# Bias transposes spread over four steps, and the retention's transposes and halves set one step later

## The chip, the cores and the metric

The kernel runs on one core of one Trainium2 chip. The metric is the device time of one execution in microseconds, from a profile-free timing; three runs of the kernel before are given. The profile is one further execution, recorded by the hardware profiler.

## The reference, cut to what matters

One layer of a streaming encoder: x (256 frames of 2048 channels) passes a SwiGLU feed-forward block, then a mixing stage, then a second feed-forward block and a last norm. All of it is float32. Only the mixing stage matters here:

```
proj = rmsnorm(x) @ w_in                       # q_a k_a v_a q_r k_r v_r g_r gate_a gate_r
scores = q_a k_a^T * hd**-0.5 + bias           # 8 heads of 128; bias = rel_bias[clip(q - k)]
att = softmax(masked scores) v_a               # chunks of 64 frames see earlier chunks only
q_r, k_r = rotary(q_r), rotary(k_r)
ret = (q_r k_r^T * decay) v_r                  # 8 heads, no softmax
ret = silu(g_r) * ret / rms(ret)               # rms over one head's 128 channels
merged = sigmoid(gate_a) * (att @ w_out_att) + sigmoid(gate_r) * (ret @ w_out_ret)
x = x + merged @ w_out
```

## The kernel before, in words

**Products in three parts.** Every large product splits both operands into a high and a low float32r part and multiplies three times (`three`, lines 130 to 132: high by high, low weight by high, high weight by low). Weights come in blocks of 256 rows by 512 columns on SyncE's queue (`fetch`, L116), ScalarE rounds a block to its high part (L122), and VectorE subtracts it to get the low part (L123).

**Steps.** A step is one such weight block. An ordinary step (`standard`) multiplies it with both frame tiles t = 0 and 1, first all six matmuls of t = 0 into one accumulator bank, then six of t = 1 into another. Before the matmuls of step c, `run` first issues the split of the weight block of step c + 3 (four split buffers, so this split waits for the end of step c - 1 on TensorE), and then the functions that are due in step c. `later(n, fn)` puts a function into the list of the step that is n steps after the current one; a list is worked off in the order in which its entries were made. All engines take their instructions in this order, so the order of the work is written out by these calls and nothing reorders it. When the last step of a job is issued, its `done` function is called, which evicts the accumulators.

**Banks.** TensorE writes to eight PSUM banks in three groups: three with the tag acc, three with the tag z (`acc_tile`), and two side banks (`side_tile`). A new tile gets a bank of its tag when one of those before it has been read for the last time; its first matmul waits for that on TensorE, in front of all later matmuls.

**The stretch in question.** The mixing stage's projection to the second half of v_r begins at the step called `mixed` in the code; here the steps are counted from it, so that `mixed` is step 0. The order of jobs is: v_r second half, steps 0 to 7; q_r heads 0 to 3, 8 to 15; k_r heads 0 to 3, 16 to 23; q_r heads 4 to 7, 24 to 31; k_r heads 4 to 7, 32 to 39; then att @ w_out_att, four jobs of four steps (blocks 0 to 3 of the result's columns), 40 to 55; ret @ w_out_ret, four jobs of four steps, 56 to 71; and merged @ w_out from 72. Each job of steps 40 to 71 takes one bank acc for t = 0 and one bank z for t = 1; attention's are evicted by VectorE (`branch_a_done`, L1027, into siga).

Small work is hung into these steps:

- The bias. Its transposed table is read from DRAM in two tiles (biasT, four heads each). `bias_natural` runs in step 0: for each pair of heads four transposes on TensorE into a side bank (psb, L326) and a copy by ScalarE (L331); at the end VectorE fills the corner that is masked (L333).
- Attention, head h of 8: the scores in step 4 + 4h (L854, L855 into the side bank as; VectorE's scaling plus bias at L862 reads it), exponentials in step 5 + 4h, the division in 6 + 4h, the transposes of the weights in step 8 + 4h (L890 into the side bank apt, copied by ScalarE at L892), the values in step 10 + 4h (L898, L899 into the side bank av, split by L343 and L344).
- The retention's queries and keys. `ret_qk_done` runs at the end of step 15 (q_r, heads 0 to 3: qr0), 23 (kr0), 31 (qr1) and 39 (kr1). ScalarE scales the two accumulators, VectorE turns them (rotary, L815 to L818) one and two steps later, and `to_transposed` transposes them four steps later (19, 27, 35, 43): four transposes per frame tile into a side bank (qr0p and so on, L349), copied by ScalarE for t = 0 (L784) and by VectorE for t = 1 (L786).
- The retention itself, `retention(b)`, for heads 4b to 4b + 3, is put into the lists at the end of kr0 (step 23) and kr1 (step 39). RET_WAIT is (14, 5). Scores of head i: L923, L924 into the side bank rs, multiplied with the decay by VectorE (L926, L927 into rp), in steps 37, 39, 41, 43 for b = 0 and 44, 46, 48, 50 for b = 1. Values three steps later (L936 to L938), all four heads into one pair of accumulators (ro, one bank acc and one bank z), which are taken with the first head's values, in step 40 and step 47. `finish` runs in step 46 and step 53: ScalarE squares the accumulators, VectorE sums the squares (L948), GpSimd takes the power (L340), and VectorE scales the accumulators by it and by the gate (rg, L954), first for t = 0, then for t = 1. Three steps later, in step 49 and step 56, `ret.put` transposes the result (retp, L349), ScalarE rounds it to the high part (reth, L343) and VectorE subtracts (retl, L344).
- The result of heads 0 to 3 is block 0 of the operand ret and is used from step 56 on; that of heads 4 to 7 is block 1 and is first used in step 58.

The lines that set these distances:

```
HALF_K = D // P // 2
RET_WAIT = (14, 5)
...
            to_transposed(key, b, srcs, 4)
...
            later(3, lambda: [ret.put(b, t, srcs[t]) for t in range(NT)])

        for i in range(4):
            for s, stage in enumerate(head(i)):
                later(wait + 2 * i + 3 * s, stage)
        later(wait + 2 * 4 + 1, finish)
```

Of the kernel before, what the change touches and what calls it, by code (L numbers as in the profile page):

```python
# [15 lines left out]
P = 128  # L16
SEQ = 256
NT = SEQ // P
D = 2048
DFF = 5632  # L20
CHUNK = 64
HEADS = 8
# [7 lines left out]
MASKED = -1e30  # L30
# [7 lines left out]
HALF_K = D // P // 2  # L38
LEAD = 12
MIX_LEAD = 8  # L40
RET_WAIT = (14, 5)
HELD = 6

SHARE = (0.85,) * 4 + (1.0,) * 4 + (0.8,) + (0.4,) * 3 + (0.15,) * 4
# [27 lines left out]
def block_kernel(ctx: ExitStack, tc: tile.TileContext, x, g1, w1g, w1u, w1d, gm, w_in, rel, woa, wor, wo,  # L72
                 g2, w2g, w2u, w2d, gf, cos, sin, decay, ident, out):
    nc = tc.nc
# [10 lines left out]
    def act_tile(dt, name):  # L85
        return apool.tile([P, 4, SEQ], dt, tag="act", name=name)

    def acc_tile(name, tag="acc"):
        return psum.tile([P, NB], F32, tag=tag, name=name, bufs=3)

    def side_tile(name):
        return psum.tile([P, NB], F32, tag="side", name=name, bufs=2)

    def tmp_tile(name, tag="t", bufs=None):
        return tmp.tile([P, NB], F32, tag=tag, name=name, bufs=bufs)
# [9 lines left out]
    def later(n, fn):  # L105
        due.setdefault(state["step"] + n, []).append(fn)
# [151 lines left out]
    def load_gain(g, i, queue=nc.gpsimd):  # L258
        rows = small.tile([D // P, P], F32, tag="rows", name=f"grows{i}", bufs=1)
        queue.dma_start(rows, g[0].rearrange("(k p) -> k p", p=P))  # L260

        def turn():
            ps = side_tile(f"gps{i}")
            nc.tensor.transpose(ps[:, : D // P], rows, id_sb[: D // P, : D // P])
            nc.vector.tensor_copy(gains[:, i, :], ps[:, : D // P])

        return turn
# [8 lines left out]
    table = {}  # L276
# [42 lines left out]
    def bias_natural(bt):  # L319
        for b in range(HEADS // 4):  # L320
            table["bias", b] = act_tile(F32, f"bias{b}")
        for h in range(0, HEADS, 2):
            ps = side_tile(f"psb{h}")
            for i in range(2):
                for j in range(2):
                    nc.tensor.transpose(  # L326
                        ps[:, (2 * i + j) * P : (2 * i + j + 1) * P],
                        bt[(h + i) // 4][:, (h + i) % 4, j * P : (j + 1) * P],
                        id_sb,
                    )  # L330
            nc.scalar.copy(table["bias", h // 4][:, h % 4 : h % 4 + 2, :].rearrange("p h k -> p (h k)"), ps)  # L331
        for b in range(HEADS // 4):
            nc.vector.memset(table["bias", b][0:CHUNK, :, CHUNK:P], MASKED)  # L333


    def rsqrt(dst, ssum, n, width):

        v = small.tile([P, width], F32, tag="v", name="v")
        nc.vector.tensor_scalar(v, ssum, 1.0 / n, EPS, op0=ALU.mult, op1=ALU.add)
        nc.gpsimd.tensor_tensor(dst, v, mhalf[:, :width], op=ALU.pow)  # L340
# [5 lines left out]
    def transpose4(src, name):  # L346
        ps = side_tile(name)
        for i in range(4):
            nc.tensor.transpose(ps[:, i * P : (i + 1) * P], src[:, i * P : (i + 1) * P], id_sb)  # L349
        return ps  # L350
# [421 lines left out]
    def heads_t(ts):  # L772
        return slice(ts * P, (ts + 1) * P)

    def to_transposed(key, b, srcs, steps):

        dst = act_tile(F32, f"{key}{b}T")
        tposed[key, b] = dst

        def go():  # L780
            for t in range(NT):
                ps = transpose4(srcs[t], f"{key}{b}p{t}").rearrange("p (i q) -> p i q", i=4)
                if t == 0:
                    nc.scalar.copy(dst[:, :, heads_t(t)], ps)  # L784
                else:
                    nc.vector.tensor_copy(dst[:, :, heads_t(t)], ps)  # L786

        later(steps, go)
# [12 lines left out]
    def ret_qk_done(key, b, after=None):  # L801
        def done(acc):
            srcs = []
            half = HD // 2

            def turn(t, s):
                r = tmp_tile(f"{key}{b}{t}r", "qk", 4)
                u = tmp_tile(f"{key}{b}{t}u", "scaled", 1)
                s4 = s.rearrange("p (h j d) -> p h j d", h=4, j=2)
                r4 = r.rearrange("p (h j d) -> p h j d", h=4, j=2)  # L810
                u4 = u.rearrange("p (h j d) -> p h j d", h=4, j=2)
                c = cos_sb[:, t, :].unsqueeze(1).to_broadcast([P, 4, half])
                n = sin_sb[:, t, :].unsqueeze(1).to_broadcast([P, 4, half])
                for j in range(2):
                    nc.vector.tensor_mul(r4[:, :, j, :], s4[:, :, j, :], c)  # L815
                    nc.vector.tensor_mul(u4[:, :, j, :], s4[:, :, 1 - j, :], n)
                nc.vector.tensor_sub(r4[:, :, 0, :], r4[:, :, 0, :], u4[:, :, 0, :])
                nc.vector.tensor_add(r4[:, :, 1, :], r4[:, :, 1, :], u4[:, :, 1, :])  # L818
                srcs.append(r)


            for t in range(NT):
                s = tmp_tile(f"{key}{b}{t}", "gate", 2)
                nc.scalar.activation(s, acc[t], AF.Copy, scale=nm.scale(t))
                later(1 + t, lambda t=t, s=s: turn(t, s))
            to_transposed(key, b, srcs, 4)
            if after is not None:
                after()

        return done  # L830
# [13 lines left out]
    ret = Operand("ret", HEADS // 4)  # L844
# [65 lines left out]
    def retention(b):  # L910

        wait = RET_WAIT[b]
        outs = {}

        def head(i):
            h = 4 * b + i
            hs = slice(i * HD, (i + 1) * HD)
            sm = {}

            def scores():  # L920
                q, k = tposed["qr", b], tposed["kr", b]
                ps = side_tile(f"rs{h}")
                nc.tensor.matmul(ps[:, 0:SEQ], k[:, i, 0:P], q[:, i, :], start=True, stop=True)  # L923
                nc.tensor.matmul(ps[:, SEQ : SEQ + P], k[:, i, P:SEQ], q[:, i, P:SEQ], start=True, stop=True)  # L924
                s = act_tile(F32, f"rp{h}").rearrange("p a q -> p (a q)")[:, : 3 * P]
                nc.vector.tensor_mul(s[:, :SEQ], ps[:, :SEQ], table["decay", b][:, i, :])  # L926
                nc.vector.tensor_mul(s[:, SEQ:], ps[:, SEQ : SEQ + P], table["decay", b][:, i, 0:P])  # L927
                sm["s"] = s

            def values():  # L930
                if i == 0:
                    for t in range(NT):
                        outs[t] = acc_tile(f"ro{b}{t}", ("acc", "z")[t])
                v = nat["vr", b]
                s = sm["s"]
                nc.tensor.matmul(outs[0][:, hs], s[:, 0:P], v[:, 0, hs], start=True, stop=True)  # L936
                nc.tensor.matmul(outs[1][:, hs], s[:, P:SEQ], v[:, 0, hs], start=True, stop=False)
                nc.tensor.matmul(outs[1][:, hs], s[:, SEQ:], v[:, 1, hs], start=False, stop=True)  # L938

            return scores, values  # L940

        def finish():
            srcs = []
            for t in range(NT):
                sq = tmp_tile(f"rsq{b}{t}", "gate", 2)
                nc.scalar.activation(sq, outs[t], AF.Square)
                ms = small.tile([P, 4], F32, tag="ms", name="ms")
                nc.vector.reduce_sum(ms, sq.rearrange("p (h d) -> p h d", h=4), axis=AX.X)  # L948
                rs = small.tile([P, 4], F32, tag="rs", name="rs")
                rsqrt(rs, ms, HD, 4)  # L950
                o = tmp_tile(f"rg{b}{t}", "qk", 4)
                for i in range(4):
                    hs = slice(i * HD, (i + 1) * HD)
                    nc.vector.scalar_tensor_tensor(  # L954
                        o[:, hs], outs[t][:, hs], rs[:, i : i + 1], nat["gr", b][:, t, hs], op0=ALU.mult, op1=ALU.mult
                    )
                srcs.append(o)
            later(3, lambda: [ret.put(b, t, srcs[t]) for t in range(NT)])

        for i in range(4):  # L960
            for s, stage in enumerate(head(i)):
                later(wait + 2 * i + 3 * s, stage)
        later(wait + 2 * 4 + 1, finish)

    w_in0 = w_in[0]
# [129 lines left out]
    turn = load_gain(g1, 0, nc.scalar)  # L1095
# [41 lines left out]
    def set_bias():  # L1137
        bt = bias_transposed()
        later(4, lambda: bias_natural(bt))
# [75 lines left out]
```

## Time and profile before

| what | value |
|---|---|
| median of three runs | 2105.22 us (2102.99 to 2106.69) |
| the profiled execution's own time | 2105.12 us |
| its span, first to last instruction | 2103.4 us |
| mean granted clock of TensorE | 0.998 of full speed |
| TensorE busy (matmuls) | 2065.5 us, 98% |
| VectorE, ScalarE, GpSimd busy | 1761.1, 1408.4, 273.8 us (84%, 67%, 13%) |
| HBM traffic | 224 GB/s over the span |
| chain of work that ended last | TensorE 77%, VectorE 11%, issue 4%, ScalarE 4%, DMA 3% |

The stretch that the change touches lies between about 1070 and 1270 us of the span. In the rows, a line of the timeline gives the start of an instruction (or of several merged ones) in us from the span's start, its duration in us, engine, line of the kernel, operation, what it writes and reads, and how many were merged; in brackets stands the idle time ahead of it and what ended that. Matmuls are pipelined, so durations of neighbours overlap, and the distance between starts is the rate. PEclk is the granted clock of TensorE as a share of full speed.

### The profile page before, as it was taken

The page shows a single profiled execution, that of the slowest core. Times are in us where ns is not written, and L with a number is a line of the kernel's source. Part 1 is how long each engine was busy: PE and PEld are TensorE (multiplying, and loading weights), DVE is VectorE, ACT ScalarE, POOL GpSimd, SP SyncE. Part 2 cuts the span into 40 slices and gives each one's busy share as a digit, 9 for nine tenths or more (in the row PEclk, how much of TensorE's full clock was granted, in tenths as well). Part 3 has the DMA queues.
Part 4 walks back from the last instruction along what each step waited for, and adds up shares of the span by engine and source line. Part 5 has one row for each costly group of instructions (what it writes and reads, how often), then busy time and mean ns, then how long its engine had stood idle before and what let it go on. Part 6 is the DMA issues. An engine that isn't in the chain of part 4 may idle for free.

```text
span 2103.4 us, 25824 instructions
## 1 busy us (share of the span) xinstructions
PE 2065.5 (98%) x9256; PEld 1688.7 (80%) x9256; DVE 1761.1 (84%) x1825; ACT 1408.4 (67%) x1734; POOL 273.8 (13%) x322
## 2 busy tenths in 40 slices
PE   9999999999999999999999999999999999999998
PEld 7788878888888888878778888887888778888886
DVE  6998899888988799889966667568888988898986
ACT  7677667777777766766664434556776677677785
POOL 1111211122111110121100000010122012110200
PEclk9999999999999999999999999999999999999999
DMA  8667876788678777798776645575787668766873
GB/s 300 192 215 231 276 208 209 229 265 239 197 234 236 244 210 238 255 289 247 220 253 180 214 137 184 187 241 172 229 277 231 192 223 268 236 199 228 279 210 130
DMA packets 219313, 473.27 MB, mean 225 GB/s; under 512 B 14816, under 2 KB 15568, under 8 KB 219184
## 3 DMA queue, kind: packets, MB, share of 16 engines
q1 hardware_dynamic: 161376, 310.42, 44.0%
q0 software_dynamic: 54752, 155.88, 27.4%
q10 hardware_dynamic: 3056, 5.32, 0.7%
q8 instruction: 72, 1.18, 0.2%
q14 instruction: 57, 0.47, 0.1%
HBM read 462.65 MB, written 8.91 MB: 224 GB/s over the span
## 4 chain that ended last, share of the span: by engine, by line
PE 77%; DVE 11%; issue 4%; ACT 4%; DMA 3%; ACTq 0%; POOL 0%; POOLq 0%; DVEq 0%
PE acc L131 15%; PE acc L132 14%; PE acc L130 14%; DVE lo L123 2%; DMA raw<-in_ffn_w_down_dram 2%; ACT hi L122 1%; DMA z992x<-in_ffn_w_gate_dram 1%; DMA rawz24323r<-in_ffn_w_up_dram 1%; ACT xall L733 0%; PE z128a L131 0%; PE z800a L131 0%; PE z205a L130 0%; PE z380a L130 0%; PE z128a L130 0%; PE z800a L130 0%
## 5 line engine op out<-in xcount | busy, mean ns | idle before, releaser
L123 DVE TENSOR_TENSOR lo<-raw,hi 128x1024 fp32r<-128x1024 f32 (+1 forms) x401 | 487.2, 1217 | 176.5 <-ACT hi L122 174.7
L122 ACT CAST hi<-raw 128x1024 fp32r<-128x1024 f32 (+1 forms) x401 | 418.9, 1048 | 230.0 <-PE acc L132 143.7
L730 ACT ACTIVATE acc<-xall 128x512 f32<-128x512 f32 x96 | 57.5, 599 | 8.4 <-DVE f1g L697 3.5
L733 ACT ACTIVATE xall<-acc 128x512 f32<-128x512 f32 x96 | 56.4, 588 | 4.5 <-PE acc L132 3.8
L130 PE MATMUL acc<-hi,mgh 128*128 128x512 f32 x128 | 50.1, 392 | 0.0
L132 PE MATMUL acc<-hi,mgl 128*128 128x512 f32 x128 | 49.8, 389 | 0.0
L131 PE MATMUL acc<-lo,mgh 128*128 128x512 f32 x128 | 49.8, 389 | 0.0
L131 PE MATMUL acc<-lo,nma01h 128*128 128x512 f32 x96 | 38.0, 396 | 1.6 <-DVE lo L123 1.6
L130 PE MATMUL acc<-hi,nma00h 128*128 128x512 f32 x96 | 38.9, 405 | 0.0
L131 PE MATMUL acc<-lo,nma00h 128*128 128x512 f32 x96 | 38.4, 400 | 0.3 <-DVE lo L123 0.3
L130 PE MATMUL acc<-hi,nma01h 128*128 128x512 f32 x96 | 38.5, 401 | 0.0
L132 PE MATMUL acc<-hi,nma00l 128*128 128x512 f32 x96 | 38.0, 396 | 0.0
L130 PE MATMUL acc<-hi,nma10h 128*128 128x512 f32 x96 | 37.7, 393 | 0.0
L131 PE MATMUL acc<-lo,nma10h 128*128 128x512 f32 x96 | 37.6, 392 | 0.0
L132 PE MATMUL acc<-hi,nma01l 128*128 128x512 f32 x96 | 37.6, 391 | 0.0
L132 PE MATMUL acc<-hi,nma10l 128*128 128x512 f32 x96 | 37.5, 390 | 0.0
L132 PE MATMUL acc<-hi,nma11l 128*128 128x512 f32 x96 | 37.4, 390 | 0.0
L130 PE MATMUL acc<-hi,nma11h 128*128 128x512 f32 x96 | 37.4, 390 | 0.0
L131 PE MATMUL acc<-lo,nma11h 128*128 128x512 f32 x96 | 37.4, 389 | 0.0
L132 PEld LDWEIGHTS acc<-hi,mgl 128*128 128x128 f32 x128 | 24.0, 188 | 4.9
L130 PEld LDWEIGHTS acc<-hi,mgh 128*128 128x128 f32 x128 | 24.0, 188 | 4.9
L131 PEld LDWEIGHTS acc<-lo,mgh 128*128 128x128 f32 x128 | 24.0, 188 | 4.9
(6130 smaller groups left out, 7143.9 us busy)
## 6 DMA issues: line engine op xcount, KB each, us to landing
raw<-in_ffn_w_down_dram SPq DMA_DIRECT2D x176, 512.0 KB, 6.2
raw<-in_w_in_dram SPq DMA_DIRECT2D x96, 512.0 KB, 4.4
raw<-in_ffn_w_up_dram SPq DMA_DIRECT2D x32, 512.0 KB, 8.6
raw<-in_w_out_dram SPq DMA_DIRECT2D x32, 512.0 KB, 3.7
raw<-in_ffn_w_gate_dram SPq DMA_DIRECT2D x31, 512.0 KB, 5.7
raw<-in_w_out_att_dram SPq DMA_DIRECT2D x16, 512.0 KB, 3.9
raw<-in_w_out_ret_dram SPq DMA_DIRECT2D x16, 512.0 KB, 3.9
z380x<-in_w_in_dram POOLq DMA_DIRECT2D x8, 512.0 KB, 7.8
```

The costliest lines, as they stand in the source:

```text
L122: nc.scalar.copy(hi[:, p, :], raw[:, p, :])
L123: nc.vector.tensor_sub(lo[:, p, :], raw[:, p, :], hi[:, p, :].bitcast(F32))
L130: nc.tensor.matmul(acc, ahi, whi, start=first, stop=False, **more)
L131: nc.tensor.matmul(acc, ahi, wlo, start=False, stop=False, **more)
L132: nc.tensor.matmul(acc, alo, whi, start=False, stop=last, **more)
L730: nc.scalar.activation(acc, xs[t][:, cols], AF.Copy, scale=2.0)
L733: nc.scalar.activation(xs[t][:, cols], acc, AF.Copy, scale=0.5)
```

## The change

The turn of the bias is split: the pair of heads 0 and 1 is transposed in step 0, pairs 2, 4 and 6 in steps 1, 2 and 3, each with its own masked fill. RET_WAIT becomes (15, 6), so that both halves of the retention (scores, values, finish) start a step later: b = 0 has scores in 38, 40, 42, 44, values in 41, 43, 45, 47 and its finish in 47; b = 1 has scores in 45, 47, 49, 51, values in 48, 50, 52, 54 and its finish in 54. `to_transposed` of the retention's queries and keys runs five steps after the projection's end: 20, 28, 36, 44. `ret.put` runs four steps after its finish, so in 51 and 58. No transfer is added or moved, and the amount of computation is the same.

```diff
--- before.py
+++ after.py
@@ -38,7 +38,7 @@
 HALF_K = D // P // 2
 LEAD = 12
 MIX_LEAD = 8
-RET_WAIT = (14, 5)
+RET_WAIT = (15, 6)
 HELD = 6
 
 SHARE = (0.85,) * 4 + (1.0,) * 4 + (0.8,) + (0.4,) * 3 + (0.15,) * 4
@@ -319,7 +319,8 @@
     def bias_natural(bt):
         for b in range(HEADS // 4):
             table["bias", b] = act_tile(F32, f"bias{b}")
-        for h in range(0, HEADS, 2):
+
+        def turn(h):
             ps = side_tile(f"psb{h}")
             for i in range(2):
                 for j in range(2):
@@ -328,9 +329,13 @@
                         bt[(h + i) // 4][:, (h + i) % 4, j * P : (j + 1) * P],
                         id_sb,
                     )
-            nc.scalar.copy(table["bias", h // 4][:, h % 4 : h % 4 + 2, :].rearrange("p h k -> p (h k)"), ps)
-        for b in range(HEADS // 4):
-            nc.vector.memset(table["bias", b][0:CHUNK, :, CHUNK:P], MASKED)
+            dst = table["bias", h // 4][:, h % 4 : h % 4 + 2, :]
+            nc.scalar.copy(dst.rearrange("p h k -> p (h k)"), ps)
+            nc.vector.memset(dst[0:CHUNK, :, CHUNK:P], MASKED)
+
+        turn(0)
+        for h in range(2, HEADS, 2):
+            later(h // 2, lambda h=h: turn(h))
 
 
     def rsqrt(dst, ssum, n, width):
@@ -823,7 +828,7 @@
                 s = tmp_tile(f"{key}{b}{t}", "gate", 2)
                 nc.scalar.activation(s, acc[t], AF.Copy, scale=nm.scale(t))
                 later(1 + t, lambda t=t, s=s: turn(t, s))
-            to_transposed(key, b, srcs, 4)
+            to_transposed(key, b, srcs, 5)
             if after is not None:
                 after()
 
@@ -955,7 +960,7 @@
                         o[:, hs], outs[t][:, hs], rs[:, i : i + 1], nat["gr", b][:, t, hs], op0=ALU.mult, op1=ALU.mult
                     )
                 srcs.append(o)
-            later(3, lambda: [ret.put(b, t, srcs[t]) for t in range(NT)])
+            later(4, lambda: [ret.put(b, t, srcs[t]) for t in range(NT)])
 
         for i in range(4):
             for s, stage in enumerate(head(i)):
```

## Rows read from the trace of the kernel before

**Rows 1.** The page's busy table: engine, busy us, share, instructions.

```profile
PE 2065.5 (98%) x9256; PEld 1688.7 (80%) x9256; DVE 1761.1 (84%) x1825; ACT 1408.4 (67%) x1734; POOL 273.8 (13%) x322
```

**Rows 2.** Waits of TensorE, 1069 to 1265 us: total, times, longest.

```profile
PE psb L326 <- ACT bias L331: 1.9, 1, 1.9
PE retp L349 <- DVE rp L927: 1.0, 1, 1.0
PE kr1p L349 <- ACT kr1T L784: 0.7, 1, 0.7
...
```

**Rows 3.** Timeline of TensorE, steps 0 and 1.

```profile
1069.95 1.04 PE L326 MATMUL psb<-id_sb,biasT 128*128 128x128 f32 x8
1072.84 1.15 PE L326 MATMUL psb<-id_sb,biasT 128*128 128x128 f32 x8 [1.85 <-ACT bias L331]
1073.74 0.63 PE L130 MATMUL acc<-hi,nma00h 128*128 128x512 f32 x1
...
1078.16 0.39 PE L130 MATMUL acc<-hi,nma00h 128*128 128x512 f32 x1
...
1080.88 0.39 PE L130 MATMUL acc<-hi,nma01h 128*128 128x512 f32 x1
```

**Rows 4.** Windows of TensorE: busy us, PEclk, DMA share, GB/s.

```profile
1238.00:1244.00 6.00, 4.97 (x30) 1.00 0.72 212
1073.74:1077.20 3.46, 3.46 (x12) 0.52 0.97 335
```

**Rows 5.** Timeline of TensorE, step 19.

```profile
1132.91 0.60 PE L349 MATMUL qr0p<-id_sb,qr00r 128*128 128x128 f32 x4
1134.11 0.66 PE L349 MATMUL qr0p<-id_sb,qr01r 128*128 128x128 f32 x4 [0.60 <-DVE attl L344]
1134.52 0.48 PE L130 MATMUL acc<-hi,nma01h 128*128 128x512 f32 x1
```

**Rows 6.** Timeline of TensorE, ScalarE and VectorE, step 28.

```profile
1164.23 0.49 PE L890 MATMUL apt<-id_sb,p 128*128 128x128 f32 x3
...
1165.13 0.47 PE L130 MATMUL acc<-hi,nma00h 128*128 128x512 f32 x1
...
1165.43 0.47 ACT L892 COPY p<-apt 128x384 f32<-128x384 f32 x1
...
1166.70 0.68 DVE L862 SCALAR_TENSOR_TENSOR p<-as,bias 128x128 f32<-128x128 f32 x3
```

**Rows 7.** Timeline of TensorE and VectorE, steps 46 and 47.

```profile
1226.71 0.38 PE L936 MATMUL ro<-vr,rp 128*128 128x128 f32 x2
...
1231.37 0.48 PE L130 MATMUL acc<-hi,atth 128*128 128x512 f32 x1
...
1231.16 1.12 DVE L954 SCALAR_TENSOR_TENSOR rg<-ro,rs,gr 128x128 f32<-128x128 f32 x4 [1.15 <-POOL rs L340]
...
1234.21 1.13 DVE L954 SCALAR_TENSOR_TENSOR rg<-ro,rs,gr 128x128 f32<-128x128 f32 x4 [1.12 <-POOL rs L340]
```

**Rows 8.** Timeline of TensorE and VectorE, step 50.

```profile
1243.15 0.59 PE L923 MATMUL rs<-qr1T,kr1T 128*128 128x256 f32 x2
...
1245.91 0.28 DVE L927 TENSOR_TENSOR rp<-rs,decay 128x128 f32<-128x128 f32 x1
```

**Rows 9.** Timeline of TensorE, VectorE and ScalarE, steps 53 to 56.

```profile
1253.14 0.38 PE L936 MATMUL ro<-vr,rp 128*128 128x128 f32 x2
...
1262.02 1.03 PE L349 MATMUL retp<-id_sb,rg 128*128 128x128 f32 x8
...
1260.61 1.13 DVE L954 SCALAR_TENSOR_TENSOR rg<-ro,rs,gr 128x128 f32<-128x128 f32 x4 [1.12 <-POOL rs L340]
1261.65 2.35 DVE L123 TENSOR_TENSOR lo<-raw,hi 128x1024 fp32r<-128x1024 f32 x2
1263.92 1.28 DVE L1027 TENSOR_TENSOR siga<-acc,siga 128x512 f32<-128x512 f32 x2
...
1263.18 1.07 ACT L343 CAST reth<-retp 128x512 fp32r<-128x512 f32 x2
```

## The prediction

> **What bounds the kernel now.** I read four views. The page's busy table comes first: TensorE is busy for 98% of the span [rows 1], so a change pays only where TensorE stands still or runs slowly. The list of TensorE's waits in the stretch that the change touches comes next [rows 2]: six waits, and each is for a PSUM side bank that a slower engine still has to empty. They are 1.9 us at the bias, 1.0 at the retention's first result (retp), 0.7 at kr1p, and 0.60 three times (qr0p, whose wait stands in [rows 5], kr0p and qr1p): 5.4 us in all. The change moves exactly these six places. Third, TensorE in order of time around the bias shows a second loss [rows 3]: sixteen transposes and a wait fill 1069.95 to 1073.74, and the first eight products that follow are 0.43 us apart where ordinary ones are 0.23 apart. The windows view names it: the granted clock is 0.52 there, the 1.2 GHz level [rows 4]. Last I followed, step by step, who empties the banks that the moved work will ask for.
>
> A step of twelve products takes 2.72 us (1078.16 to 1080.88) [rows 3]; a group of four transposes takes 0.41 (1134.11 to 1134.52) [rows 5]. Steps are numbered as in the description above.
>
> **The bias.** Now step 0 lasts from 1069.95 to 1078.16, 8.21 us [rows 3]; 2.72 are products, 5.49 are the price of the turn. Afterwards one group of four stands in each of steps 0 to 3, 0.41 each plus about 0.08 for the slower first product behind it, 2.0 in all. Each step then needs one side bank, and the copy that frees it has a step's time. Gain **3.5 us**; at the least 1.85, the wait alone. Head 0's scores come at step 4, heads 4 to 7 from step 20, so no score waits for a bias. ScalarE has the same four copies; four smaller fills replace two on VectorE, which waits for ScalarE in these steps anyway; without that cover they cost what the two cost now, about half a microsecond in all.
>
> **Queries and keys, steps 19, 27, 35, 43 to 20, 28, 36, 44.** Steps 20 and 28 already hold an attention head's transposes and the next head's scores, so four side tiles now share two banks. Take step 28 as it is: transposes at 1164.23, products at 1165.13, that is 0.90 in; ScalarE's copy frees the first bank at 1165.90 (1.67 in), VectorE's scaling frees the second at 1167.38 (3.15 in) [rows 6]. The first group can start at 1.7 and end at 2.1; the second needs either the second bank or the first again. A copy behind a first group let the next group start after about 1.3 (0.41 for its transposes, some 0.2 until their end is told, 0.7 the wait at kr1p [rows 2]; the 0.2 is what 1.20 from group to group leaves beside 0.41 and a wait of 0.60 [rows 5]), so 3.0; products follow at 3.4 in place of 0.90, 2.5 more. Taken away is 1.61 (1132.91 to 1134.52) [rows 5] and a little for one break fewer: **+0.8 each, +1.6**. If the banks are handed out the other way round, both groups wait for 3.15 and it is +1.3 each. At step 36 only the head's transposes are in the way: the second group waits to 1.7, products at 2.1 where now three transposes (0.3, three quarters of a group) and 1.61 are paid apart, **+0.2**. Step 44 repeats step 43 (scores, then keys): 0. So these four waits are not lost: VectorE's late release is replaced by a fuller step.
>
> **The retention's first half, steps 37 to 46 become 38 to 47.** No transfer moves with it; GpSimd's power, in the finish, stands behind loads issued long before; the weights' queue is not passed. What moves is the release of its accumulators. The tags acc and z have three banks each. At step 48 the second half's results take one and the third branch job of attention (woa, block 2) another; a third still holds branch job 1, which is multiplied out only after the finish. So block 2 must take the banks of the first half's results, and these are free when the finish has scaled them. In the finish's step now (1226.71 its start), they are free at 1232.28 and 1235.34, 5.57 and 8.63 in; the next step's products start at 1231.37, 4.66 in [rows 7]. Today block 2 starts a step after that (step 48, finish in 46), past both. Afterwards it starts in the step next to the finish: its first product waits from 4.66 to 5.6, 0.95, and six products (1.36) later the z bank is still held, from 6.98 to 8.65, 1.67. **+2.65**; nothing if I misread who holds the third bank. Queued behind these products is everything on TensorE.
>
> **Its transposes, step 49 to 51.** They come behind the last scores (now in step 50). Those are two products as in an attention head, 0.6 (0.90 less three transposes [rows 6]), and VectorE frees their bank at 1246.19, 3.04 after their start [rows 8]. The first group of four goes from 0.6 to 1.0 into the other bank; the second waits until 3.05 and ends at 3.46. Now scores and transposes cost 0.6 and 2.05 apart: two groups, the wait of 1.0 [rows 2] and the 0.2 ahead of it. **+0.8**.
>
> **The second half's, step 56 to 58.** Now they have two steps until block 1 of the result is multiplied, in step 58. Afterwards they stand directly ahead of those products. The finish ends 8.60 after the start of its step (1253.14 to 1261.74) [rows 9]; it will be step 54. Step 58 starts 0.6 + 4 x 2.72 = 11.5 after that start (0.6 for the results' matmuls: of the 4.66 in [rows 7], 2.72 are products and 0.6 scores, and the rest is two such blocks). VectorE, after 8.60, has step 55's split (1.15), two multiplications of the branch (1.2), three more splits, the last to about 14.4, and then the lows, 0.64 each [rows 9]: the first at 15.0. Its first high is ready 1.7 after the transposes' start, at 13.2, by ScalarE's pair now (1262.02; 1263.18, half of 1.07) [rows 9]. TensorE ends its eight transposes at 12.3, waits 0.9, makes two products, and waits from 13.65 to 15.0 for the low. **+2.3**; between 0.9, if VectorE has caught up and only the high is late, and 2.6.
>
> **Small terms.** Steps 38 and 52 take two blocks of small work where two steps took one each: -0.2. Buffers of the bias, queries, keys and results live one to three steps longer; four buffers hold the results, and the gate loads that wait for tiles are far ahead. Zero, with a microsecond as the outer bound, the wait at retp [rows 2].
>
> **The sum** without the clock is -3.5 + 1.6 + 0.2 + 2.65 + 0.8 + 2.3 - 0.2 = +3.9. The clock comes on top. Eight products at 0.43 in place of 0.23 cost 1.6 us [rows 3]. It fell after 1.85 us of wait amid transposes, and stayed at 1.00, the 2.4 GHz level, through the wait at retp and behind it [rows 2, 4]. The new waits of about 2 us (step 48, two within 4 us; step 51; step 58, two within 4 us) lie at the first of these rather than the second. I take one fall in the three places, +1.6, with none and three as ends. From the profiled execution's 2105.1, which is the median of the runs within 0.1, that is **2110.6**.
>
> **Rivals.**
> *The accumulators are free* (step 48). If block 2 finds a bank, or the finish is done earlier, 2.65 goes and with it a place for the clock: 2105.1 + 1.25 = 2106.4, no change. It decides at whether the result's scaling ends before the products 4.66 in; rows 7 say it does not, by 0.95 and by 4.0 for the other bank's release, less six products.
> *All six waits go and none comes.* Then 3.5 + 1.8 + 0.7 + 1.0 = 7.0 is gained, 2098.1, faster. For it: each wait is on an engine that a step more lets finish. Against it: two side banks for four tiles in steps 20 and 28, a row that I can read off [rows 6]; it would need the heads' banks back within 0.90.
> *The clock falls at every new wait.* Steps 20, 28, 48, 51 and 58: 3.9 + 5 x 1.6, 2117. For it stands the fall at the bias, against it the unbroken 1.00 around retp and 0.60 waits without any fall [rows 2, 4, 5]. The Trainium skill, TensorE: Matmul & The Clock Gate, section on psum-queue depth-cycling, says that a TensorE that idles briefly between groups while it cycles through PSUM banks can swing between its two clock levels; that speaks against this change. By that rule the result is this rival's; the trace agrees once in six waits.
>
> **How the numbers follow.** The forecast, waits as summed and one fall or none, 0.50: 2109.0 to 2110.6, a microsecond or so either way for the bounds above. Clock at two to five places, 0.20: 2112 to 2117. Accumulators free, 0.18: 2105 to 2108. All waits gone, 0.07: 2098. The last 0.05 is for something unseen on either side, most of it no change. A measurement here tells about 0.2% from no change, 4.2 us, so the bounds are 2101.0 and 2109.4. Slower: 0.20 and three quarters of 0.50, with a little of the rest: 0.58. Faster: 0.07. No change: 0.35. The range 2104.5 to 2115.5 holds the first three cases but for the top of the second.
>
> **What would show it.** Right: no wait at psb, no clock of 0.52 near 1074; qr0p and kr0p waiting twice, first for ScalarE's copy of the head's transposes; a product of step 48 waiting for rg (VectorE), twice; retp's second group waiting about 2 us for rp; a product of step 58 waiting for reth, then retl. Wrong: step 48's products starting straight behind the results' matmuls, or the ret products of step 58 finding their lows, which puts the time at no change; and a clock at 1.00 throughout takes 1.6 off.

## The result, and the profile after

| what | before | changed |
|---|---|---|
| median of the runs taken together | 2103.18 us (9 runs, 2101.67 to 2106.69) | 2109.67 us (9 runs, 2107.55 to 2113.03) |
| ratio of the two | | 1.0025, 95% interval 1.0016 to 1.0033 |
| span of the profiled execution | 2103.4 us | 2107.9 us |

By the ratio the change makes the kernel slower by 0.25%, some 5.3 us (3.4 to 6.9 by the interval); the two medians alone lie 6.5 us apart. One of the eleven executions of first14, an experiment below, took 2574.82 us at a granted clock of 0.75 and is left out of its ratio.

TensorE's waits in the same stretch, line by line, were six ([rows 2] and two more like the one in [rows 5]) and are now the ones below. The lines of the code have moved down by five from the bias on, so L354 is the old L349.

The waits of TensorE in the changed kernel, 1066 to 1275 us (line waited for: us in total, times, longest):

```profile
PE acc L130 <- DVE rg L959: 2.2, 2, 1.4
PE retp L354 <- DVE rp L932: 1.8, 1, 1.8
PE acc L132 <- DVE retl L349: 0.9, 1, 0.9
PE qr1p L354 <- ACT p L897: 0.8, 1, 0.8
PE acc L130 <- ACT reth L348: 0.7, 1, 0.7
PE qr0p L354 <- ACT qr0T L789: 0.7, 1, 0.7
PE kr0p L354 <- ACT kr0T L789: 0.7, 1, 0.7
PE kr1p L354 <- ACT kr1T L789: 0.7, 1, 0.7
PE qr0p L354 <- ACT p L897: 0.6, 1, 0.6
PE kr0p L354 <- ACT p L897: 0.6, 1, 0.6
```

The bias is gone from the list, and every other place that was moved is still on it: eleven waits and 9.7 us where six and 5.4 stood. qr0p and kr0p now wait twice each, and like qr1p for ScalarE's copies in place of VectorE's attl; kr1p waits as before, and retp longer, for the same rp. Ahead of products (acc) three releasers stand where there was no wait at all (rg, reth, retl).

The stretches themselves show in the windows of TensorE (busy us, PEclk, DMA share, GB/s): steps 0 to 3, step 51, step 58, step 48.

```profile
1070.48:1083.27 12.79, 12.79 (x66) 1.00 0.92 292
1245.24:1251.57 6.33, 4.49 (x26) 1.00 0.53 167
1269.66:1275.45 5.79, 4.17 (x22) 1.00 0.83 264
1232.23:1238.39 6.16, 3.91 (x19) 1.00 0.21 71
```

Steps 0 to 3 are busy without a gap at full clock (against [rows 3, 4]); steps 51, 58 and 48 are idle for 1.8, 1.6 and 2.3 us. The clock is 1.00 in all four.

**Step 28**, in order of time, with ScalarE's two copies (compare [rows 5, 6]):

```profile
1160.32 0.49 PE L895 MATMUL apt<-id_sb,p 128*128 128x128 f32 x3
...
1162.04 0.65 PE L354 MATMUL kr0p<-id_sb,kr00r 128*128 128x128 f32 x4 [0.58 <-ACT p L897]
1163.37 0.66 PE L354 MATMUL kr0p<-id_sb,kr01r 128*128 128x128 f32 x4 [0.68 <-ACT kr0T L789]
1163.78 0.48 PE L130 MATMUL acc<-hi,nma00h 128*128 128x512 f32 x1
...
1161.51 0.47 ACT L897 COPY p<-apt 128x384 f32<-128x384 f32 x1
1162.73 0.58 ACT L789 COPY kr0T<-kr0p 128x512 f32<-128x512 f32 x1 [0.74 <-PE kr0p L354]
```

The first group of kr0p starts 1.72 us into the step, when the copy of the head's transposes has freed a bank (1161.51 + 0.47), the second when the first group's own copy has, and the products 3.46 in, where 3.4 was forecast.

**Step 48**, TensorE and VectorE (compare [rows 7]):

```profile
1232.23 0.38 PE L941 MATMUL ro<-vr,rp 128*128 128x128 f32 x2
...
1233.89 0.47 PE L130 MATMUL acc<-hi,atth 128*128 128x512 f32 x1 [0.83 <-DVE rg L959]
...
1236.93 0.47 PE L130 MATMUL acc<-hi,atth 128*128 128x512 f32 x1 [1.42 <-DVE rg L959]
...
1232.61 1.13 DVE L959 SCALAR_TENSOR_TENSOR rg<-ro,rs,gr 128x128 f32<-128x128 f32 x4 [1.16 <-POOL rs L345]
...
1235.66 1.12 DVE L959 SCALAR_TENSOR_TENSOR rg<-ro,rs,gr 128x128 f32<-128x128 f32 x4 [1.12 <-POOL rs L345]
```

Both products that open block 2 of attention's output start just behind the end of a scaling of the retention's first half (1233.74 and 1236.78): they wait for its accumulators.

**Step 51** (compare [rows 8]), TensorE and the instruction on VectorE that it waits for:

```profile
1245.24 0.59 PE L928 MATMUL rs<-qr1T,kr1T 128*128 128x256 f32 x2
...
1245.89 0.60 PE L354 MATMUL retp<-id_sb,rg 128*128 128x128 f32 x4
1248.33 0.66 PE L354 MATMUL retp<-id_sb,rg 128*128 128x128 f32 x4 [1.84 <-DVE rp L932]
...
1247.99 0.28 DVE L932 TENSOR_TENSOR rp<-rs,decay 128x128 f32<-128x128 f32 x1
```

**Step 58** (compare [rows 9]):

```profile
1269.66 1.03 PE L354 MATMUL retp<-id_sb,rg 128*128 128x128 f32 x8
1271.44 0.50 PE L130 MATMUL acc<-hi,reth 128*128 128x512 f32 x1 [0.75 <-ACT reth L348]
...
1273.04 0.50 PE L132 MATMUL acc<-hi,retl 128*128 128x512 f32 x1 [0.87 <-DVE retl L349]
...
1267.70 1.28 DVE L1032 TENSOR_TENSOR siga<-acc,siga 128x512 f32<-128x512 f32 x2
1268.90 3.49 DVE L123 TENSOR_TENSOR lo<-raw,hi 128x1024 fp32r<-128x1024 f32 x3
1272.30 1.28 DVE L349 TENSOR_TENSOR retl<-retp,reth 128x512 fp32r<-128x512 f32 x2
```

VectorE comes to the lows only at 1272.30, behind the branch's two multiplications and three splits.

Taking the distance from the first instruction of one step to that of a later one in both timelines gives the bill of the two profiled executions:

| steps | before, us | changed, us | difference | forecast |
|---|---|---|---|---|
| 0 to 3, bias | 16.38 | 12.79 | -3.59 | -3.5 |
| 19 and 20, qr0 | 8.17 | 9.03 | +0.86 | +0.8 |
| 27 and 28, kr0 | 8.19 | 9.03 | +0.84 | +0.8 |
| 35 and 36, qr1 | 7.55 | 7.68 | +0.13 | +0.2 |
| 37 to 54, first half | 65.05 | 68.52 | +3.47 | +2.65 + 0.8 - 0.2 |
| 55 to 58, second half's transposes | 11.78 | 13.95 | +2.17 | +2.3 |
| 0 to 74, all of it | 248.22 | 252.06 | +3.84 | +3.9, and +1.6 for the clock |

The spans differ by 0.7 us beyond that, of which 0.5 lie before step 0 (1070.48 against 1069.95). The runs differ by 5.3 us where the table has 3.8, without the fall of the clock that the forecast added. The interval of the runs holds both numbers, so it cannot tell them apart; the experiments show what was particular about the profiled execution of the kernel before.

### The profile page after: what moved, and what is told of

The parts are those of the page before. It is cut to its first block, busy times and chain, and to the rows that moved or that the text cites. A ratio compares the mean times of both kernels' runs of the same rounds, so it can differ in the third digit from the quotient of the medians.

```text
span 2107.9 us, 25822 instructions
## 1 busy us (share of the span) xinstructions
PE 2063.3 (98%) x9256; PEld 1686.6 (80%) x9256; DVE 1761.0 (84%) x1827; ACT 1407.7 (67%) x1734; POOL 273.5 (13%) x322
## 4 chain that ended last, share of the span: by engine, by line
PE 76%; DVE 11%; issue 4%; ACT 4%; DMA 3%; POOL 0%; ACTq 0%; POOLq 0%; DVEq 0%
PE acc L131 15%; PE acc L132 14%; PE acc L130 14%; DVE lo L123 2%; DMA raw<-in_ffn_w_down_dram 2%; ACT hi L122 1%; DMA z992x<-in_ffn_w_gate_dram 1%; DMA rawz24323r<-in_ffn_w_up_dram 1%; ACT xall L738 0%; PE z800a L131 0%; PE z380a L130 0%; PE z877a L130 0%; PE z800a L130 0%; PE z380a L132 0%; PE z877a L132 0%
## 5 line engine op out<-in xcount | busy, mean ns | idle before, releaser
L130 PE MATMUL acc<-hi,atth 128*128 128x512 f32 x64 | 26.3, 411 | 2.2 <-DVE rg L959 2.2
```

The source lines that it names most:

```text
L130: nc.tensor.matmul(acc, ahi, whi, start=first, stop=False, **more)
```

## The experiments

All edits are against the kernel named; ratios are to the kernel before, timed on the same chip.

**The bias alone** (bias_only), on the kernel before:

```diff
-        for h in range(0, HEADS, 2):
+        def turn(h):
...
+        turn(0)
+        for h in range(2, HEADS, 2):
+            later(h // 2, lambda h=h: turn(h))
```

> Only the bias turn is spread over steps 0 to 3; the retention keeps its old steps. Theory (each part pays by its own waits, and they add up): steps 0 to 3 shrink by 3.6 us as they do in the changed kernel, the clock stays at 1.00 near 1074, and the six-wait list keeps its five others (qr0p, kr0p, qr1p, kr1p, retp); 3.6 us faster than before, ratio about 0.9983. Rival (only the wait itself is recovered, and a transposes' slow clock comes back elsewhere): 1.9 us faster, ratio 0.9991.

Measured: 0.9990 (0.9981 to 0.9999), medians 2102.36 and 2104.31. The window of steps 0 to 3 is the changed kernel's to the hundredth:

```profile
1072.26:1085.05 12.79, 12.79 (x66) 1.00 0.93 298
```

The five other waits are the old ones, and all steps from 4 on have their old lengths within 0.05 us. So the theory holds for what is removed in these two profiles. The runs show a gain of 2.1 us (0.2 to 4.0), nearer to the rival's number than to 3.6, but the interval holds both. The next runs show why the two can differ.

**The moves alone** (moves_only), on the kernel before: RET_WAIT (15, 6), the transposes of queries and keys five steps after, those of the results four.

```diff
-RET_WAIT = (14, 5)
+RET_WAIT = (15, 6)
...
-            to_transposed(key, b, srcs, 4)
+            to_transposed(key, b, srcs, 5)
...
-            later(3, lambda: [ret.put(b, t, srcs[t]) for t in range(NT)])
+            later(4, lambda: [ret.put(b, t, srcs[t]) for t in range(NT)])
```

> The bias stays in step 0; the retention's transposes and halves move as in the change. Theory: the four stretches cost what they cost in the changed kernel, 0.85 and 0.83 for steps 19/20 and 27/28, 0.13 for 35/36, 3.5 for steps 46 to 54, 2.2 for the last transposes; 7.4 us slower than before, ratio about 1.0035, and the clock falls to about 0.5 behind the bias again. Rival (the spread bias pulls the rest forward and so makes part of the new waits): fewer or shorter waits than in the changed kernel, 4 to 5 us slower, ratio about 1.0022.

Measured: 1.0034 (1.0021 to 1.0046), 7 us. Each moved stretch is as long as in the changed kernel within 0.02 us, so the spread bias makes none of the new waits and hides none. One expectation failed: the clock did not fall behind the bias, although the wait there is the same. Its timeline of TensorE in step 0, and the window behind:

```profile
1069.39 1.03 PE L326 MATMUL psb<-id_sb,biasT 128*128 128x128 f32 x8
1072.29 1.14 PE L326 MATMUL psb<-id_sb,biasT 128*128 128x128 f32 x8 [1.86 <-ACT bias L331]
1073.19 0.48 PE L130 MATMUL acc<-hi,nma00h 128*128 128x512 f32 x1
```

```profile
1073.10:1076.60 3.50, 3.50 (x19) 1.00 1.00 344
```

Nineteen matmuls fall into 3.5 us where the kernel before had twelve at 0.52 [rows 4] (the last transposes of the bias are counted in both); steps 0 to 3 took 14.78 us, 1.6 less. Nothing that the moves touch comes before them.

**The kernel before, profiled four more times** (before_look1 to before_look4), for this question, no edit.

> The kernel before, looked at once more. Theory (the fall of the clock behind the bias depends on the execution, not on the order of the work alone): steps 0 to 3 take either 16.4 us with a clock near 0.5, as in its first profile, or 14.8 us with 1.00, as with the moved retention; seen over several looks, both. Rival (the retention's moves, which come later, or another lasting difference of the program made the clock stay up there): 16.4 us and the fall in every look.

> As in the look before: 14.8 us without a fall or 16.4 us with one in steps 0 to 3, by the theory not the same in all looks; by the rival 16.4 us each time.

> The kernel before again, for how often the clock falls behind the bias. So far two executions with the bias in step 0 have the fall (16.4 us in steps 0 to 3) and two have not (14.8). Theory (it depends on the execution): one of these two values. Rival (the fall is the rule, and the two without it were exceptions of those executions): 16.4 us.

> As in the look before: 14.8 or 16.4 us in steps 0 to 3 by the theory, 16.4 us by the rival.

Measured: 16.39, 14.81, 14.77 and 14.80 us in steps 0 to 3. The windows behind the bias in the first, third and fourth of these profiles:

```profile
1072.90:1076.40 3.50, 3.50 (x12) 0.55 1.00 345
```

```profile
1074.60:1078.10 3.50, 3.50 (x18) 1.00 0.96 329
```

```profile
1071.60:1075.10 3.50, 3.50 (x18) 1.00 0.96 301
```

With the first profile and the moves alone that is six executions with the same wait of 1.8 to 1.9 us amid sixteen transposes, and the clock fell to the 1.2 GHz level in two of them. The second profile has no fall there either (its records show a granted clock of 0.95 in every stretch, with products 0.23 us apart as elsewhere; that is left unexplained). The fall depends on the execution, and the first profile of the kernel before, on which the forecast rests, was one of the less usual ones. The chip alone does not decide it: the first two of the four profiles were taken on the same chip, one with the fall and one without. Without the fall the bill of the change reads -2.0 for the bias and +5.4 in all, against the third and fourth (252.06 to 246.65 and 246.63 over steps 0 to 74).

**The changed kernel, profiled once more** (after_look), no edit.

> The changed kernel again, for whether its clock ever falls at the new waits. Theory (a wait of up to 1.8 us with ordinary products close by leaves the clock up): 1.00 in steps 0 to 3, 48, 51 and 58, steps 0 to 58 as long as in its first profile within 0.2 us. Rival (it falls there in some executions, as behind the bias): a clock near 0.5 behind one of them, 1.6 us more.

Steps 0 to 74 take 252.09 us against 252.06, every stretch of the table within 0.03, and the granted clock is 1.00 through all of them. The theory holds as far as two executions go, and a third with the same late waits (the moves alone) agrees.

**The bias in four banks** (four_banks), on the kernel before: the last two groups use accumulator banks, so all sixteen transposes stay in step 0 without a wait.

```diff
-            ps = side_tile(f"psb{h}")
+            ps = acc_tile(f"psb{h}", "acc" if h == 4 else "z") if h > 2 else side_tile(f"psb{h}")
```

> The kernel before, with the third and fourth group of the bias in a bank of the tag acc and one of the tag z, so that all sixteen transposes stay in step 0 and none of them waits for a side bank. Theory (the bank's wait is what the turn costs over its transposes): steps 0 to 3 take 12.7 us, 2.0 to 2.1 less than the kernel before without a fall of the clock, and the clock stays at 1.00. Rival (sixteen transposes in a row lower the clock by themselves): 14.3 us, with a clock near 0.5 for eight products.

In one profile the transposes run through, and steps 0 to 3 take 12.68 us at full clock.

```profile
1069.50 1.91 PE L326 MATMUL psb<-id_sb,biasT 128*128 128x128 f32 x16
1071.16 0.47 PE L130 MATMUL acc<-hi,nma00h 128*128 128x512 f32 x1
```

```profile
1069.49:1082.17 12.68, 12.68 (x65) 1.00 0.88 277
```

So the wait for a side bank was what the turn could save without a fall of the clock, 2.1 us; spread over four steps the same transposes take 0.1 more (12.79). One execution does not show that sixteen transposes in a row never lower the clock.

**The first half a step earlier** (first14), on the changed kernel:

```diff
-RET_WAIT = (15, 6)
+RET_WAIT = (14, 6)
```

> The changed kernel with only the retention's first half put back by a step (RET_WAIT 14, 6). Theory (step 48's job of attention must take the accumulators that the first half's result still holds): both waits of its products for rg are gone, 2.7 us; the result's transposes come in step 50, no longer behind the last scores, and lose their wait of 1.8 us and its latency, 2.0 us; the scores and kr1p no longer share a step, 0.9 us. 5.6 us under the changed kernel, about level with the kernel before or up to 0.5 us under it, ratio 1.000. Rival (the products wait in step 48 because VectorE is behind, whichever job holds the banks): the waits for rg stay at half or more, 2 to 3 us under the changed kernel, ratio 1.0012.

Measured: 1.0005 (0.9996 to 1.0014). In the trace 5.5 us are gone against the changed kernel: step 48 takes 3.45 in place of 6.16, and the waits from 1200 us on are down to those of step 58.

```profile
PE acc L132 <- DVE retl L349: 0.9, 1, 0.9
PE acc L130 <- ACT reth L348: 0.7, 1, 0.7
```

Step 48 in this kernel, with products straight behind the results' matmuls:

```profile
1230.44 0.38 PE L941 MATMUL ro<-vr,rp 128*128 128x128 f32 x2
...
1231.02 0.48 PE L130 MATMUL acc<-hi,atth 128*128 128x512 f32 x1
```

The second half still takes its accumulators in step 48 and VectorE has the same work; only the first half's finish is a step earlier, and both waits for rg are gone entirely. That is the theory's outcome and not the rival's.

**The results' transposes three steps after the finish** (put3), on the changed kernel:

```diff
-            later(4, lambda: [ret.put(b, t, srcs[t]) for t in range(NT)])
+            later(3, lambda: [ret.put(b, t, srcs[t]) for t in range(NT)])
```

> The changed kernel with only the results' transposes put back to three steps after the finish (50 and 57). Theory: without the last scores ahead of them the first half's transposes wait for nothing (2.0 us less), and the second half's come a step ahead of their use, so that the wait for reth goes and the wait for retl stays at about 1.0 us (1.1 us less); the two waits for rg in step 48 stay at 0.8 and 1.4. 3.2 us under the changed kernel, 2 us over the kernel before, ratio about 1.001. Rival (VectorE's queue is late in step 58 anyway, whenever the transposes are made): the wait in step 58 stays at 1.6 us in all, only 2.0 us under the changed kernel, ratio 1.0015.

Measured: 1.0006 (0.9997 to 1.0016). Steps 0 to 74 are 3.13 us shorter than in the changed kernel: 2.05 in steps 49 to 54 and 1.11 in 55 to 58. Its waits from 1200 us on:

```profile
PE acc L130 <- DVE rg L959: 2.2, 2, 1.4
PE acc L132 <- DVE retl L349: 0.7, 1, 0.7
PE kr1p L354 <- ACT kr1T L789: 0.7, 1, 0.7
```

reth and retp are gone and retl stays, as in the theory, at 0.7 where about 1.0 was expected. The wait in step 48 stays the same wherever the transposes are.

**Two groups in two steps** (best), the bias spread as in the change and everything else on the kernel before:

```diff
+        for t in range(NT):
+            later(steps[t], lambda t=t: go(t))
...
+            to_transposed(key, b, srcs, (3, 4) if (key, b) == ("kr", 1) else (4, 6))
...
+            for t in range(NT):
+                later(3 + 2 * t * (1 - b), lambda t=t: ret.put(b, t, srcs[t]))
```

> The spread bias on the kernel before, with the two groups of four transposes of each retention operand set in different steps: queries and keys t = 0 four steps and t = 1 six steps after the projection (kr1: three and four), the first half's result t = 0 three and t = 1 five steps after its finish; everything else in its old step. Theory (a wait goes only where the moved group finds a side bank already read): none of the six waits is left and none comes, since no step asks for more than two side banks; 3.6 us at the bias where the clock had fallen and 2.0 where it had not, 0.8 each at qr0p, kr0p, qr1p and kr1p, 1.2 at retp. Some 6.4 to 7.9 us under the kernel before, ratio about 0.9967. Rival (another wait takes the place of each, as in the change): 2 to 3 us under the kernel before, like the spread bias alone, ratio 0.999.

Measured: 0.9968 (0.9955 to 0.9980), medians 2098.09 and 2104.71, 6.7 us faster by the ratio. The list of TensorE's waits between 1064 and 1280 us is empty. The two groups of qr0p stand in steps 19 and 21, on either side of the head's transposes that they met in the change, and neither waits:

```profile
1128.70 0.60 PE L354 MATMUL qr0p<-id_sb,qr00r 128*128 128x128 f32 x4
...
1135.65 0.60 PE L354 MATMUL qr0p<-id_sb,qr01r 128*128 128x128 f32 x4
```

Steps 0 to 74 take 240.15 us, 8.1 under the kernel before's first profile and 6.5 under before_look3 and before_look4. All six waits could be removed by placing; the change moved them to where other tiles held the banks.

## Why the prediction was right

**The forecast held in direction and in the waits that cause it**: 2110.6 was forecast and 2109.67 measured. In the difference, 5.5 us were forecast and 5.3 measured by the ratio. That both agree so closely is partly luck: the forecast started from 2105.1, the nine runs of the kernel before gave 2103.18, and two of its terms were wrong and cancel (below). The queries and keys, step 44 (no change), the retention's accumulators, its transposes in step 51 and those in step 58 were each forecast within some 0.2 us of what the trace shows (step 48's two stretches of waiting were written down as 0.95 and 1.67, which make 2.62 and not 2.65), and each of these waits has the releaser that was named: ScalarE's copies in steps 20 and 28, rg twice in step 48, rp in step 51, reth and then retl in step 58. The moves alone show that they add up. The two put-backs remove the waits of steps 48, 51 and, in part, 58; those of queries and keys go only in the last experiment, together with all others.

**The largest cost** was the wait in step 48, of which the trace of before shows nothing. There the two products that open block 2 come 2.5 and 0.9 us after the scalings that free their banks (1232.28 and 1235.34 by [rows 7]):

```profile
1234.79 0.47 PE L130 MATMUL acc<-hi,atth 128*128 128x512 f32 x1
...
1236.26 0.39 PE L130 MATMUL acc<-hi,atth 128*128 128x512 f32 x1
```

The forecast of the wait came from counting who holds three banks of one tag when the finish moves and the next job does not. Putting only that half back took both waits away; the rival that the accumulators are free is out.

**Two steps failed, and they cancel.** "Gain 3.5 us" for the bias took the slow products of [rows 3] for part of the turn. They are part of some executions: in four of six the same turn cost 1.6 less, and against those the gain is 2.0. The bound "at the least 1.85, the wait alone" was the better number. And "I take one fall in the three places, +1.6" was wrong: in the two profiles of the changed kernel and in that of the moves alone the clock stays at 1.00 through all new waits, up to 1.84 us long. Taken together the gain was put 1.5 too high and a cost of 1.6 was added that did not come, so the sum is nearly the measured one: -2.0 + 7.4 = +5.4, against 5.3 from the runs. That the total agreed is no support for the clock's part of the reasoning.

**The rivals.** All waits gone and none coming was ruled out by step 28 for this change, and is what the last experiment reaches by another placing. A clock that falls at each wait, for which the Trainium skill was cited (TensorE: Matmul & The Clock Gate, on psum-queue depth-cycling), did not happen: bank waits of 0.6 to 1.8 us in steps 20, 28, 48 and 51, and no fall in three executions. Behind the bias, the one place where the clock fell, it did so in two of six executions, so the trace agrees with the page there in part; that the cycling through banks is the reason was not shown.

## What to carry to other kernels

A wait for a buffer tells who was late; before the waiting step is moved, list for its new place how many tiles of that tag are alive there and when each is read for the last time. Moving a stage also moves the release of what it holds, and the job that takes the buffer next may not move with it. When four small tiles must pass through two banks, put them into different steps rather than all of them one step later. And a slow-clock stretch seen in one profile should be looked for in a second one before it is booked as a gain.

## What had not been expected

The fall of the clock behind the bias is not a property of the program: the same sixteen transposes and the same wait (1.8 to 1.9 us) were followed by 0.52 and 0.55 in two executions and by no fall in four. A wait of 1.84 us in step 51, with scores ahead of it and four transposes on either side, left it at 1.00 in three executions out of three. At the bias 3.79 us of transposes and wait lie between two ordinary products; in step 51 it is 3.50 us from the start of the scores to the first product. What decides between these was not tried further.
